# Output projections of the FFNs and the mLSTM: one 512-column product for both activation parts in place of two of 256 columns

## The chip, the cores and the metric

The kernel runs on one core of one Trainium2 chip. The metric is the device time of one execution in microseconds. The kernel before was run three times; the median is 1103.17 us (1102.94 to 1103.98).

## The reference

The reference is a two-layer network on 256 tokens of width 1024. Each layer has three sub-layers, and each sub-layer adds its gated output to the residual stream `x`; shift, scale and gate come from a modulation vector that is computed from the condition `c`.

```python
mod = (c_act @ ada_w[layer] + ada_b[layer]).reshape(bsz, N_SUB, 3, D_MODEL)[:, :, :, None, :]
def modulate(t, sub):
    return rms_norm(t, norm_g[layer, sub]) * (1.0 + mod[:, sub, 1]) + mod[:, sub, 0]
h = modulate(x, 0)
x = x + HALF_STEP * (1.0 + mod[:, 0, 2]) * swiglu(h, ffn_w_gate[layer, 0], ffn_w_up[layer, 0], ffn_w_down[layer, 0])
h = modulate(x, 1)
...
x = x + (1.0 + mod[:, 1, 2]) * y.astype(x.dtype)
h = modulate(x, 2)
x = x + HALF_STEP * (1.0 + mod[:, 2, 2]) * swiglu(h, ffn_w_gate[layer, 1], ffn_w_up[layer, 1], ffn_w_down[layer, 1])
```

`y` is the output of a hybrid mixer (a recurrent unit and a state-space block) in the first layer, and of an mLSTM block in the second. `swiglu` is `(silu(h @ w_gate) * (h @ w_up)) @ w_down` with an inner width of 2816. Everything is float32. The change touches the last product of four FFNs, `... @ w_down` (2816 to 1024), and that of the mLSTM (2048 to 1024).

## The kernel before

**Layout.** Activations lie with features on partitions and the 256 tokens (T) along the free axis. A width of 1024 is 8 chunks (ND) of 128 features, the FFN's inner width 22 (NF). The sub-layers have numbers s = 0 to 5: FFN, hybrid, FFN, FFN, mLSTM, FFN.

**Precision.** Each float32 factor is split into an upper and a lower part of the program's type fp32r. Activations are split into a tile `both` of shape [128, 2, 256]: `both[:, 0]` is the upper part, `both[:, 1]` the lower one, one behind the other in memory (L359, L360). Weights come as pieces of eight 128x128 tiles, 512 KB each: a DMA on SP's queue brings `wraw`, ScalarE casts it to `whi` (L99), VectorE subtracts and leaves `wlo` (L100). Pieces are made four ahead of their use; four raw buffers and six pairs of parts hold them. A weight tile then takes three products (`multiply`): upper weights by upper activations (L372), upper weights by lower activations (L373), lower weights by upper activations (L374). All three have 256 columns and add up in one half of a bank of 512 float32 columns. Each product loads its weights anew (a LDWEIGHTS on the row called PEld, beside the product before it).

**Output projection** (`out_project`). For the FFNs and the mLSTM it runs over eight output chunks d; each takes one of four banks (`mm_bank`), `project` runs over all input tiles (22 tiles `ph` in an FFN, 16 tiles `yb` in the mLSTM), and then:

- VectorE scales the bank by the gate and adds it to `x` (L492),
- ScalarE squares the new `x` (L349), VectorE adds up the squares (L353),
- ScalarE and VectorE make the next sub-layer's input from `x` times its scale, split into two parts `hb` (L418, L419).

The hybrid (s = 1) takes another path of the same function, through `banks`, which the change leaves alone. VectorE also computes the modulation: blocks `ada` of 128x1024 (L230) are handed out over the weight pieces by a table.

**Start of the next sub-layer** (`begin`). The first 32 weight tiles of a sub-layer are multiplied with the not yet normalised input (258 columns, L434 to L436), while the norm is made: products of one column sum the squares (`rst_n`, L317), VectorE computes the reciprocal root (L283 to L292), TensorE spreads it (`rsb_n`, L340), and VectorE and ScalarE write the normalised `hb` (L402 to L405). `rst_n` needs the square of the last chunk of `x`, so the last chunk of a projection stands ahead of the next norm.

**Order.** The program is traced in the order of the code; a scheduler then decides the order on each engine. Each engine executes its own list in order, and waits at an instruction whose inputs are not there.

Of the kernel before, what the change touches and what calls it, by code (L numbers as in the profile page):

```python
# [15 lines left out]
ALU = mybir.AluOpType  # L16
# [4 lines left out]
T = 256  # L21
D = 1024
ND = D // P
# [111 lines left out]
def body(ctx: ExitStack, tc: tile.TileContext, a, out, dbg=None):  # L135
    nc = tc.nc
# [21 lines left out]
    def mm_bank(name):  # L158
        return ps_mm.tile([P, 512], F32, tag="mm", name=name)
# [18 lines left out]
    xs_t = [xall[:, k, :] for k in range(ND)]  # L178
# [23 lines left out]
    for b in range(2):  # L202
        q = fpool.tile([P, D], F32, tag="xsq", name=f"xsq{b}")
        squares = nc.vector.scalar_tensor_tensor(out=q, in0=xn[:, b], scalar=1.0, in1=xn[:, b], op0=ALU.mult,
                                                 op1=ALU.mult, accum_out=ss_in[:, b:b + 1])
# [40 lines left out]
    W = Weights(tc, a["wst"], rawp, partp, pump)  # L246
# [14 lines left out]
    def mod_gate(s, f):  # L261
        m = mods[s]
        o = COL["ada_b"] + 24 * s + 16
        g = modp.tile([P, 8], F32, tag="gate", name=f"gate{s}")
        nc.vector.tensor_tensor(out=g, in0=m[:, 16:24], in1=cols[:, o:o + 8], op=ALU.add)
        nc.vector.tensor_scalar(out=g, in0=g, scalar1=1.0, scalar2=f, op0=ALU.add, op1=ALU.mult)
        return g
# [101 lines left out]
    def multiply(dst, both, start, stop):  # L369

        wh, wl = W.next()
        m = nc.tensor.matmul(dst, wh, both[:, 0, :], start=start, stop=False, skip_group_check=True)  # L372
        nc.tensor.matmul(dst, wh, both[:, 1, :], start=False, stop=False, skip_group_check=True)  # L373
        nc.tensor.matmul(dst, wl, both[:, 0, :], start=False, stop=stop, skip_group_check=True)  # L374
        return m

    def project(dst, rhs):

        for k, both in enumerate(rhs):
            last = multiply(dst, both, k == 0, k == len(rhs) - 1)  # L380
        return last
# [27 lines left out]
    def scale_shift_columns(s):  # L409
        sh, _ = mod_shift_scale(s)  # L410
        shb = sh.unsqueeze(2).to_broadcast([P, 8, 2])
        nc.vector.tensor_copy(hh[:, :, T:T + 2], shb)
        nc.vector.tensor_tensor(out=hl[:, :, T:T + 2], in0=shb, in1=hh[:, :, T:T + 2].bitcast(F32), op=ALU.subtract)
# [42 lines left out]
    def out_project(s, rhs, half, beside=None):  # L456


        acc = [xp.tile([P, T], F32, tag=f"ssq{s % 2}", name=f"ssq{s}")]
        banks = []  # L460
        if isinstance(rhs, tuple):

            *early, rhs = rhs
            for n, (part, lo, hi) in enumerate(early):
                for d in range(ND):
                    if n < 2:
                        beside(n, d)
                    if n == 0:
                        if d % 2 == 0:
                            bank = mm_bank(f"od{s}_{d}")  # L470
                        banks.append(bank[:, d % 2 * T:(d % 2 + 1) * T])
                    dst = banks[d]
                    for k, both in enumerate(part[lo:hi]):

                        m = multiply(dst, both, n == 0 and k == 0 and d % 2 == 0, False)
                        if n == 0 and k == 0:
                            if d % 2 == 0:
                                head = m
                            else:
                                tc.add_manual_dep(m.ins, head.ins.name, NOSYNC, reason="one start per bank")  # L480
            rhs = rhs[0][rhs[1]:rhs[2]]
        for n, d in enumerate(LAST_ORDER if banks else range(ND)):
            if banks:
                dst = banks[d]
                for k, both in enumerate(rhs):
                    multiply(dst, both, False, k == len(rhs) - 1)
            else:
                dst = mm_bank(f"od{s}_{d}")[:, 0:T]
                project(dst, rhs)
            if n == 0:  # L490
                g = mod_gate(s, 0.5 if half else 1.0)
            nc.vector.scalar_tensor_tensor(out=xs_t[d], in0=dst, scalar=g[:, d:d + 1], in1=xs_t[d],  # L492
                                           op0=ALU.mult, op1=ALU.add)
            last_act = [add_square(acc, xs_t[d], n, ND, f"o{s}_{d}")]
            if s < 5:
                if n == 0:
                    scale_shift_columns(s + 1)
                scale_chunk(s + 1, d)
            elif d == 5:
                root = small.tile([P, 1], F32, tag="root", name="root", bufs=1)  # L500
                with tc.issue_after(last_act[0]):
                    nc.scalar.activation(root, eps, AF.Sqrt)
            if dbg is not None:
                nc.gpsimd.dma_start(dbg[f"x{s}"][d], xs_t[d])
        return acc
# [793 lines left out]
    rs, _ = rsqrt_act(sum_tokens(acc, "fin", "mm")[:, 0:2], "fin")  # L1299
    banks = [ax_bank(f"fin{i}", ("ax", "ax", "p", "q")[i]) for i in range(4)]  # L1300
# [5 lines left out]
    for lo in (0, 512):  # L1306
        for b in range(2):
            dst, src = res[:, b, lo:lo + 512], banks[2 * (lo // 512) + b]
# [113 lines left out]
```

## Time and profile before

| | |
|---|---|
| median of three runs | 1103.17 us |
| the profiled execution, its span | 1102.1 us |
| instructions in the span | 23364 |
| VectorE's differences `wlo` (L100) | 366, 445.4 us |
| ScalarE's casts `whi` (L99) | 364, 379.7 us |
| read from memory | 269.77 MB |

The span is the time from the first to the last instruction that the profiler saw; the time of a run is about 1.1 us longer. In the profile PE is TensorE's products, PEld its weight loads, DVE is VectorE, ACT ScalarE, SP the engine that issues the weight DMAs. Rows read: line of the code, engine, operation, result and inputs by their names in the program, shape and count; then busy time in us and mean duration in ns. A product's duration runs from its start until its last result is written, and products overlap; the pace is read from start to start. By start times the projections lie at 136 to 196 us (s = 0), 492 to 552 (s = 2), 674 to 734 (s = 3), 868 to 912 (s = 4) and 1033 to 1093 (s = 5).

### The profile page before, as it was taken

The numbers are of one execution on the slowest core, as the hardware profiler recorded it, in microseconds if no ns is written. First come the engines' busy times: TensorE is split into PE (matmuls) and PEld (weight loads), VectorE is DVE, ScalarE is ACT, GpSimd is POOL, SyncE is SP. The second block draws the span as 40 slices with busy tenths as digits, with TensorE's granted clock in tenths as the row PEclk, the third lists the DMA queues.
The fourth block names the chain that finished last, engine by engine and source line by source line (L and its number), as shares of the span: only waits on it lengthen the run. The fifth ranks groups of instructions, "written<-read, shape, count | busy, mean of one in ns | idle before, by whom it ended". The sixth has DMA issues, their size and how long they took to land.

```text
span 1102.1 us, 23364 instructions
## 1 busy us (share of the span) xinstructions
PE 1087.0 (99%) x9350; PEld 1073.5 (97%) x9350; DVE 919.7 (83%) x1651; ACT 642.5 (58%) x1051; POOL 9.4 (1%) x29
## 2 busy tenths in 40 slices
PE   8999999999999999999999999999999999999997
PEld 6999999999999999999999999999999999999997
DVE  7999998999999899989699988869778868766552
ACT  5665455677986665454554554548776655544452
POOL 0000000000000000000000000010000000000000
PEclk9999999999999999999999999999999999999999
DMA  9889998655845489999848998853432664775551
GB/s 371 329 304 388 359 384 339 193 192 191 287 159 182 152 298 369 355 344 329 281 164 317 335 328 308 311 203 116 146 95 93 201 193 164 265 234 197 194 173 39
DMA packets 74990, 272.34 MB, mean 247 GB/s; under 512 B 8417, under 2 KB 8577, under 8 KB 74882
## 3 DMA queue, kind: packets, MB, share of 16 engines
q1 hardware_dynamic: 74304, 269.49, 69.8%
q0 software_dynamic: 432, 1.10, 0.4%
q8 instruction: 73, 1.20, 0.4%
q14 instruction: 35, 0.29, 0.1%
q10 hardware_dynamic: 146, 0.27, 0.1%
HBM read 269.77 MB, written 1.05 MB: 246 GB/s over the span
## 4 chain that ended last, share of the span: by engine, by line
PE 81%; DVE 12%; ACT 2%; DMA 2%; issue 2%; SPq 0%; DVEq 0%; ACTq 0%
PE gu L373 13%; PE gu L374 13%; PE gu L372 13%; PE od L373 9%; PE od L372 9%; PE od L374 9%; DVE wlo L100 4%; DMA wraw<-in_wst_dram 1%; PE zz L373 1%; PE zz L374 1%; PE zz L372 1%; PE gu_f L434 1%; PE gu_f L436 1%; PE gu_f L435 1%; DVE ada L230 1%
## 5 line engine op out<-in xcount | busy, mean ns | idle before, releaser
L100 DVE TENSOR_TENSOR wlo<-wraw,whi 128x1024 fp32r<-128x1024 f32 x366 | 445.4, 1220 | 95.2 <-ACT whi L99 93.9
L99 ACT CAST whi<-wraw 128x1024 fp32r<-128x1024 f32 x364 | 379.7, 1049 | 229.4 <-PE od L373 71.4
L373 PE MATMUL gu<-hb,whi 128*128 128x256 f32 x1312 | 361.0, 276 | 0.4 <-DVE hb L569 0.4
L374 PE MATMUL gu<-hb,wlo 128*128 128x256 f32 x1312 | 360.7, 276 | 0.0
L372 PE MATMUL gu<-hb,whi 128*128 128x256 f32 x1312 | 358.5, 277 | 1.8 <-ACT hb L404 1.1
L372 PEld LDWEIGHTS gu<-hb,whi 128*128 128x128 f32 x1312 | 244.5, 188 | 2.8 <-ACT hb L404 1.3
L373 PEld LDWEIGHTS gu<-hb,whi 128*128 128x128 f32 x1312 | 246.3, 188 | 0.8 <-DVE hb L569 0.8
L374 PEld LDWEIGHTS gu<-hb,wlo 128*128 128x128 f32 x1312 | 246.3, 188 | 0.0
L372 PE MATMUL od<-ph,whi 128*128 128x256 f32 x704 | 194.3, 276 | 0.0
L373 PE MATMUL od<-ph,whi 128*128 128x256 f32 x704 | 194.3, 276 | 0.0
L374 PE MATMUL od<-ph,wlo 128*128 128x256 f32 x704 | 194.3, 276 | 0.0
L230 DVE SCALAR_TENSOR_TENSOR ada<-ada,cact 128x1024 f32<-128x1024 f32 x144 | 175.1, 1217 | 1.3 <-DMA ada<-in_adaT_dram 1.3
L374 PEld LDWEIGHTS od<-ph,wlo 128*128 128x128 f32 x704 | 132.2, 188 | 0.0
L372 PEld LDWEIGHTS od<-ph,whi 128*128 128x128 f32 x704 | 132.2, 188 | 0.0
L373 PEld LDWEIGHTS od<-ph,whi 128*128 128x128 f32 x704 | 132.2, 188 | 0.0
L359 ACT CAST ph<-fg 128x256 fp32r<-128x256 f32 x88 | 35.1, 408 | 106.2 <-DVE fg L516 106.2
L360 DVE TENSOR_TENSOR ph<-fg,ph 128x256 fp32r<-128x256 f32 x88 | 36.3, 420 | 12.1 <-ACT ph L359 12.1
L492 DVE SCALAR_TENSOR_TENSOR x<-od,gate,x 128x256 f32<-128x256 f32 x48 | 23.0, 481 | 26.4 <-PE od L374 26.4
L349 ACT ACTIVATE sq_o<-x 128x256 f32<-128x256 f32 x42 | 17.6, 418 | 41.4 <-DVE x L492 41.2
L373 PE MATMUL zz<-hb,whi 128*128 128x256 f32 x128 | 36.2, 283 | 0.0
L372 PE MATMUL zz<-hb,whi 128*128 128x256 f32 x128 | 36.2, 283 | 0.0
L374 PE MATMUL zz<-hb,wlo 128*128 128x256 f32 x128 | 36.2, 283 | 0.0
(412 smaller groups left out, 1948.2 us busy)
## 6 DMA issues: line engine op xcount, KB each, us to landing
wraw<-in_wst_dram SPq DMA_DIRECT2D x366, 512.0 KB, 4.6
ada<-in_adaT_dram SPq DMA_DIRECT2D x144, 512.0 KB, 5.9
xn<-in_x_dram SPq DMA_DIRECT2D x2, 512.0 KB, 4.0
wgr<-in_ml_wg_dram POOLq DMA_DIRECT2D x3, 256.0 KB, 3.0
out_dram<-res SPq DMA_DIRECT2D x3, 256.0 KB, 2.4
out_dram<-res ACTq DMA_DIRECT2D x1, 256.0 KB, 2.8
cols<-in_cols_dram SPq DMA_DIRECT2D x1, 226.0 KB, 7.6
wkr<-in_ml_wkr_dram POOLq DMA_DIRECT2D x1, 128.0 KB, 2.3
```

The source lines that it names most:

```text
L99: raw_hi = nc.scalar.copy(hi, raw)
L100: self.last = nc.vector.tensor_tensor(out=lo, in0=raw, in1=hi.bitcast(F32), op=ALU.subtract)
L230: return nc.vector.scalar_tensor_tensor(out=raw, in0=raw, scalar=1.0, in1=cact, op0=ALU.mult, op1=ALU.mult, accum_out=mods[s][:, m:m + 1])
L349: square = nc.scalar.activation(q, x, AF.Square).ins
L359: nc.scalar.copy(hi, src)
L360: nc.vector.tensor_tensor(out=both[:, 1, :], in0=src, in1=hi.bitcast(F32), op=ALU.subtract)
L372: m = nc.tensor.matmul(dst, wh, both[:, 0, :], start=start, stop=False, skip_group_check=True)
L373: nc.tensor.matmul(dst, wh, both[:, 1, :], start=False, stop=False, skip_group_check=True)
L374: nc.tensor.matmul(dst, wl, both[:, 0, :], start=False, stop=stop, skip_group_check=True)
L434: nc.tensor.matmul(dst, wh, rh, start=(k == 0), stop=False)
L435: nc.tensor.matmul(dst, wh, rl, start=False, stop=False)
L492: nc.vector.scalar_tensor_tensor(out=xs_t[d], in0=dst, scalar=g[:, d:d + 1], in1=xs_t[d], op0=ALU.mult, op1=ALU.add)
```

## The change

A new helper, `multiply_wide`, takes a whole bank. One product of upper weights by both parts of the activation (512 columns) leaves the upper parts' sum in the bank's left half and the lower parts' sum in its right half; a second product adds lower weights by upper activations to the left half. In `out_project` the first seven chunks of an FFN's or the mLSTM's projection use it; the eighth chunk stays with `multiply`. After each of the seven chunks VectorE adds the right half to `x`, in one more instruction with the same gate, and then the left half as before.

```diff
--- before.py
+++ after.py
@@ -374,6 +374,13 @@
         nc.tensor.matmul(dst, wl, both[:, 0, :], start=False, stop=stop, skip_group_check=True)
         return m
 
+    def multiply_wide(bank, both, start, stop):
+
+        wh, wl = W.next()
+        nc.tensor.matmul(bank.rearrange("p (i t) -> p i t", i=2), wh, both, start=start, stop=stop,
+                         skip_group_check=True)
+        nc.tensor.matmul(bank[:, 0:T], wl, both[:, 0, :], start=False, stop=stop, skip_group_check=True)
+
     def project(dst, rhs):
 
         for k, both in enumerate(rhs):
@@ -484,11 +491,19 @@
                 dst = banks[d]
                 for k, both in enumerate(rhs):
                     multiply(dst, both, False, k == len(rhs) - 1)
+            elif n < ND - 1:
+                wide = mm_bank(f"od{s}_{d}")
+                dst = wide[:, 0:T]
+                for k, both in enumerate(rhs):
+                    multiply_wide(wide, both, k == 0, k == len(rhs) - 1)
             else:
                 dst = mm_bank(f"od{s}_{d}")[:, 0:T]
                 project(dst, rhs)
             if n == 0:
                 g = mod_gate(s, 0.5 if half else 1.0)
+            if not banks and n < ND - 1:
+                nc.vector.scalar_tensor_tensor(out=xs_t[d], in0=wide[:, T:2 * T], scalar=g[:, d:d + 1], in1=xs_t[d],
+                                               op0=ALU.mult, op1=ALU.add)
             nc.vector.scalar_tensor_tensor(out=xs_t[d], in0=dst, scalar=g[:, d:d + 1], in1=xs_t[d],
                                            op0=ALU.mult, op1=ALU.add)
             last_act = [add_square(acc, xs_t[d], n, ND, f"o{s}_{d}")]
```

The lines move with it: what is L492 before is L507 after, and the added addition is L505; the wide product is L380, the product with the lower weights behind it L382; L418/L419 are L425/L426.

On TensorE the first FFN's projection shows what happens to the products, here two tiles of chunk 1 before (`od0_1` is the bank of chunk 1 of sub-layer 0, `ph0_4` the fifth input tile, `whi47` and `wlo47` piece 47 of the weights):

```order
L372 MATMUL od0_1_1976<-ph0_4_828,whi47_1832 128x256
L373 MATMUL od0_1_1976<-ph0_4_828,whi47_1832 128x256
L374 MATMUL od0_1_1976<-ph0_4_828,wlo47_1833 128x256
L372 MATMUL od0_1_1976<-ph0_5_834,whi47_1832 128x256
L373 MATMUL od0_1_1976<-ph0_5_834,whi47_1832 128x256
L374 MATMUL od0_1_1976<-ph0_5_834,wlo47_1833 128x256
```

The same place on TensorE after the change, three tiles:

```order
L380 MATMUL od0_1_1955<-ph0_3_822,whi47_1832 128x512
L382 MATMUL od0_1_1955<-ph0_3_822,wlo47_1833 128x256
L380 MATMUL od0_1_1955<-ph0_4_828,whi47_1832 128x512
L382 MATMUL od0_1_1955<-ph0_4_828,wlo47_1833 128x256
L380 MATMUL od0_1_1955<-ph0_5_834,whi47_1832 128x512
L382 MATMUL od0_1_1955<-ph0_5_834,wlo47_1833 128x256
```

A tile has two products in place of three, the order of tiles and pieces is the same. Four FFNs with seven chunks of 22 tiles and the mLSTM with seven chunks of 16 tiles make 728 tiles that change.

On VectorE the end of the same projection, around the addition of chunk 6, before (`wlo65` is the difference of piece 65, `ada62` a modulation block, `hb` the next input):

```order
L100 TENSOR_TENSOR wlo65_2474<-wraw65_2471,whi65_2473 128x1024
L492 SCALAR_TENSOR_TENSOR x_104<-od0_6_2458,gate0_1962,x_104 128x256
L100 TENSOR_TENSOR wlo66_2504<-wraw66_2501,whi66_2503 128x1024
L230 SCALAR_TENSOR_TENSOR ada62_2507,mod2_1836<-ada62_2507,cact_117 128x1024
L353 TENSOR_TENSOR ssq0_1870<-ssq0_1870,sq_o0_6_2550 128x256
L419 SCALAR_TENSOR_TENSOR hb_106<-x_104,scale1_1968,hb_106 128x256
```

The same place on VectorE after the change:

```order
L505 SCALAR_TENSOR_TENSOR x_104<-od0_6_2332,gate0_1940,x_104 128x256
L100 TENSOR_TENSOR wlo65_2344<-wraw65_2341,whi65_2343 128x1024
L507 SCALAR_TENSOR_TENSOR x_104<-od0_6_2332,gate0_1940,x_104 128x256
L100 TENSOR_TENSOR wlo66_2366<-wraw66_2363,whi66_2365 128x1024
L230 SCALAR_TENSOR_TENSOR ada62_2369,mod2_1836<-ada62_2369,cact_117 128x1024
L353 TENSOR_TENSOR ssq0_1870<-ssq0_1870,sq_o0_6_2403 128x256
L426 SCALAR_TENSOR_TENSOR hb_106<-x_104,scale1_1947,hb_106 128x256
```

There are two additions now, and the difference of piece 65, which stood ahead of the addition, stands between them.

A little further on VectorE, at the addition of chunk 7, the last, and the norm behind it (`rsv`, `rsy` and `rsw` are the root's chain), before:

```order
L100 TENSOR_TENSOR wlo68_2577<-wraw68_2574,whi68_2576 128x1024
L492 SCALAR_TENSOR_TENSOR x_104<-od0_7_2555,gate0_1962,x_104 128x256
L100 TENSOR_TENSOR wlo69_2607<-wraw69_2604,whi69_2606 128x1024
L419 SCALAR_TENSOR_TENSOR hb_106<-x_104,scale1_1968,hb_106 128x256
L329 TENSOR_SCALAR rsv_n1_2667<-rst_n1_2662 128x2
L723 TENSOR_SCALAR dt_3199<-cols_105 128x8
L283 TENSOR_SCALAR rsy_n1_2670<-rsv_n1_2667 128x2
L286 TENSOR_TENSOR rsw_n1_2669<-rsy_n1_2670 128x2
```

The same place on VectorE after the change:

```order
L507 SCALAR_TENSOR_TENSOR x_104<-od0_7_2408,gate0_1940,x_104 128x256
L738 TENSOR_SCALAR dt_3052<-cols_105 128x8
L100 TENSOR_TENSOR wlo68_2430<-wraw68_2427,whi68_2429 128x1024
L426 SCALAR_TENSOR_TENSOR hb_106<-x_104,scale1_1947,hb_106 128x256
L329 TENSOR_SCALAR rsv_n1_2520<-rst_n1_2515 128x2
L283 TENSOR_SCALAR rsy_n1_2523<-rsv_n1_2520 128x2
L100 TENSOR_TENSOR wlo69_2460<-wraw69_2457,whi69_2459 128x1024
L286 TENSOR_TENSOR rsw_n1_2522<-rsy_n1_2523 128x2
```

The difference of piece 68 moved behind the last addition, and that of piece 69 into the root's chain. SP's list of weight and modulation loads differs in one place, where one weight load and one modulation load have changed places.

## The prediction

> **What bounds the kernel now.** I read the page's busy shares first, then its clock line, then the chain of work that ended last, then PE's waits.
>
> ```profile
> PE 1087.0 (99%) x9350; PEld 1073.5 (97%) x9350; DVE 919.7 (83%) x1651; ACT 642.5 (58%) x1051; POOL 9.4 (1%) x29
> PEclk9999999999999999999999999999999999999999
> PE 81%; DVE 12%; ACT 2%; DMA 2%; issue 2%; SPq 0%; DVEq 0%; ACTq 0%
> L372 PE MATMUL od<-ph,whi 128*128 128x256 f32 x704 | 194.3, 276 | 0.0
> L372 PE MATMUL od<-yb,whi 128*128 128x256 f32 x128 | 35.3, 276 | 0.0
> ```
>
> TensorE is busy for 99% of the span and 81% of the chain; the clock is at full speed in every slice. The last two rows are the products that the change touches (a third of them: L373 and L374 have as many). Their idle time is 0.0, so nothing makes them wait. The kernel is bound by PE, and in these stages by the number and pace of products, not by weights or VectorE.
>
> A matmul's listed duration (276 ns) contains its pipeline; what counts is the distance from one start to the next. From the timelines of PE and of its weight loads in the first projection:
>
> ```profile
> 160.18 0.28 PE L372 MATMUL od<-ph,whi 128*128 128x256 f32 x1
> 160.29 0.28 PE L373 MATMUL od<-ph,whi 128*128 128x256 f32 x1
> 160.41 0.28 PE L374 MATMUL od<-ph,wlo 128*128 128x256 f32 x1
> ...
> 163.92 0.28 PE L372 MATMUL od<-ph,whi 128*128 128x256 f32 x1
> 160.18 0.19 PEld L373 LDWEIGHTS od<-ph,whi 128*128 128x128 f32 x1
> 160.30 0.19 PEld L374 LDWEIGHTS od<-ph,wlo 128*128 128x128 f32 x1
> ```
>
> From 160.18 to 163.92 there are 33 products (11 tiles): 3.74/33 = 113.3 ns each, **340.0 ns per tile**. Every product has a load of its own, which begins with the product before it.
>
> **What sets the 113.3 ns?** Products of other shapes tell: four float32 lines of the mLSTM in the chain, and one-column products in PE's timeline:
>
> ```profile
> 779.92 0.93 PE v L1069 x8
> 780.85 0.86 PE q L1076 x4
> 781.71 1.78 PE s L1088 x8
> 197.13 0.60 PE L317 MATMUL rst_n<-ones,sq_o 128*128 128x1 f32 x4
> 197.60 0.58 PE L317 MATMUL rst_n<-ones,ssq 128*128 128x1 f32 x4
> ```
>
> v has 136 columns and takes 0.93/8 = 116 ns; q has 256 and takes 0.86/4 = 215 ns; s has 264 and takes 1.78/8 = 222.5 ns. q's 256 columns take 1.9 times as long as the projection's 256, which I read as two passes over them. From v to q that is 99 ns for 240 column passes, 0.4125 ns each; 256 columns in one pass therefore stream in about 105.6 ns, plus a fixed part of 215/2 - 105.6 = 1.9. The two rows of rst_n (197.13 to 197.60 for four) show that products of one column still take 0.47/4 = 118 ns. So a 256-column product of the projection, at 113.3, is held by the load of its weights more than by its columns, by a margin of a few ns. A 512-column pass is as many passes as one q product: **215 ns (estimate from q)**, long enough to hide a load.
>
> **The change on PE.** 4 FFN projections x 7 chunks x 22 tiles = 616 tiles, and 7 x 16 = 112 in the mLSTM: **728 tiles**. Each loses one product and one load; its moving columns stay 768. The new pair is 215 ns for the wide product, with the load of wlo under it, then a 256-column product with the next tile's load under it. If that one stays at 113.3, the pair is 328.3, a gain of 11.7 ns per tile. But rows behind products that were bound by their stream show another pace:
>
> ```profile
> 262.04 1.02 PE L804 MATMUL st<-xw,bnat 128*128 128x512 f32 x2
> ...
> 263.01 0.28 PE L373 MATMUL xl<-hb,whi 128*128 128x256 f32 x1
> ...
> 264.80 0.28 PE L373 MATMUL xl<-hb,whi 128*128 128x256 f32 x1
> ```
>
> After the wide float32 products at 262.04 the same 256-column products run at (264.80 - 263.01)/15 = 119 ns, where the projection has 113.3. In the new tile every narrow product stands behind a wide one, so I take 119 for it: 215 + 119 = **334 ns per tile, 6 ns less than 340**. The bounds: 328 from below (113.3 stays), 344 from above (215 with 5 more for the load beside it, as the narrow ones show, and 124 as the slowest spacing, twice the same 5 over 113.3). 728 x 6.0 ns = 4.4 us gained, from 8.5 us to a loss of 2.9.
>
> **The change on VectorE.** 5 stages x 7 = 35 more scaled additions. Each chunk's first addition waits for the last product of its bank, as the old one did; the second follows it. What VectorE has free, by stage (columns: us; then busy PE, PEld, DVE, ACT, POOL with counts; clock, DMA share, GB/s):
>
> ```profile
> core 0: us, PE busy (x) PEld busy (x) DVE busy (x) ACT busy (x) POOL busy (x), PEclk, DMA share, GB/s
> 136.00:184.00 48.00, 48.00 (x426) 48.00 (x426) 46.80 (x71) 26.67 (x35) 0.00 (x0) 1.00 1.00 381
> 184.00:209.00 25.00, 24.99 (x215) 24.78 (x214) 20.28 (x45) 9.90 (x18) 0.98 (x3) 1.00 0.72 244
> 209.00:339.00 130.00, 127.85 (x1130) 124.74 (x1129) 127.28 (x257) 111.45 (x216) 0.00 (x0) 1.00 0.59 195
> 492.00:552.00 60.00, 60.00 (x532) 60.00 (x531) 48.11 (x69) 29.25 (x38) 1.07 (x2) 1.00 0.90 312
> 868.00:912.00 44.00, 44.00 (x391) 44.00 (x390) 31.20 (x41) 23.20 (x33) 0.00 (x0) 1.00 0.67 215
> 1033.00:1093.00 60.00, 60.00 (x532) 60.00 (x531) 27.14 (x33) 25.60 (x35) 0.00 (x0) 1.00 0.37 125
> 188.60 0.48 DVE L492 SCALAR_TENSOR_TENSOR x<-od,gate,x 128x256 f32<-128x256 f32 x1 [2.85 <-PE od L374]
> 189.00 1.22 DVE L100 TENSOR_TENSOR wlo<-wraw,whi 128x1024 fp32r<-128x1024 f32 x1
> ```
>
> An addition takes 0.40 us to the next start, so seven take 2.8 us. In the three later projections shown VectorE is idle for 12, 13 and 33 us: 2.8 us are hidden there, and I cost them at nothing; without that cover they would be 2.8 us per stage. The bank is held 0.4 us longer, and four banks of 7.5 us each cover it. The stages whose cover is thin are the first projection (VectorE 46.8 of 48) and the hybrid behind it (127.28 of 130). The additions eat the 2.85 us of idle time at 188.60; in the new order one weight difference less stands ahead of the first addition of od_6 and ahead of that of od_7, and wlo69, which stood ahead of the root's chain, now stands inside it. In the hybrid VectorE has almost nothing free, and so what PE gains in the first projection it loses there: 7 x 22 x 6.0 ns = **0.9 us of the gain goes**. At worst all of 2.8 us return, at best nothing.
>
> The end of the first projection is the place where a late VectorE reaches PE:
>
> ```profile
> 196.08 0.48 DVE L492 SCALAR_TENSOR_TENSOR x<-od,gate,x 128x256 f32<-128x256 f32 x1 [0.17 <-PE od L374]
> 196.48 1.22 DVE L100 TENSOR_TENSOR wlo<-wraw,whi 128x1024 fp32r<-128x1024 f32 x1
> 196.83 0.28 PE L436 MATMUL bc<-hb,wlo 128*128 128x258 f32 x1
> ```
>
> The last addition began at 196.08, after 0.17 us of waiting for its bank; ScalarE squares what it leaves, and rst_n (197.13, above) comes 0.30 us after the product before it instead of 0.12: rst_n is already the square that PE waits for. Between the additions of od_6 and od_7 the order has as many weight differences and modulation blocks as before, and one addition more: 0.40 less the 0.17 of idle time makes the last addition **0.2 us** late, and PE with it. Behind it a weight difference of 1.22 us now stands inside the root's chain; PE has the begin's products to do meanwhile (96 of 0.12 us), so I cost it at nothing; 1.2 is the upper bound of the term. ScalarE's cast, SP's queue of weight loads and the order on both stay as they are but for a swap of one weight load with one modulation load on SP. The last chunk of each stage keeps three products, so the other stages' ends keep their form.
>
> **The sum**: -4.4 + 0.9 + 0.2 = -3.3 us. The profiled span is 1102.1; the median of the runs is 1103.17, so 1.1 us lie around the span, which I leave: 1103.2 - 3.3 = **1099.9 us**.
>
> The page "TensorE: Matmul & The Clock Gate" of the Trainium skill, section "LDWEIGHTS (loading the stationary operand)", gives a load as its columns divided by 1.2 ns, 106.7 for 128; that speaks for loads as the pace, and for a narrow product that keeps it; the 119 behind wide products speaks against taking that for the whole. By the page's load alone, with the 6.6 ns that the trace has above it (113.3), the tile would be 328, and the sum that of the first rival.
>
> **The rivals.**
>
> *The narrow product stays at 113.3.* The pair is 328.3 and the gain 11.7 ns. For it: the load begins with the product before it, however that came to start. Against it: the 119 in the xl rows. All 728 tiles give 8.5 us, less 1.8 for the first projection (154 x 11.7) and 0.2 more at its end: -6.5, so 1096.7; with nothing lost, 1094.7.
>
> *Only a fixed cost per product goes.* Products would be bound by columns, at 113.3 per 256, and a wide one would take twice that less the fixed part, 1.9 ns by the q row. 728 x 1.9 = 1.4 us, less 0.3 for the first projection and 0.2 at its end: -0.9, so 1102.3, which is no change. Against it stand 215 for 512 passes in q, 11.6 less than 226.6. The same page, section "Back-to-back issue gap", has columns divided by 2.4 plus 2.5 ns for a product; by that rule three products of 256 are 327.5 and the new pair 325.0, a gain of 2.5 ns and 1.8 us; the trace's 113.3 instead of 109.2 speaks against that rule at 256 columns.
>
> *The change doesn't shorten anything*: each half of the wide product takes what a narrow product takes (113.3), and nothing is gained: +0.2 at the end of the first projection, 1103.4.
>
> *A load beside a wide stream slows both (slower).* The wide product reads two kilobytes per partition while wlo is read for the array; if it takes 220 and the narrow one 124, the pair is 344. 728 x 4 ns = +2.9, and 0.2 at the end of the first projection: 1106.3. It decides from a pair of 340 ns on. For it: 119 against 113.3 shows that loads and streams do disturb each other. Against it: q's and s's loads lie beside their streams too, at 0.4125 ns per column pass.
>
> **How the numbers follow.** Forecast (pair of 332 to 337): 0.42. Narrow stays at 113.3: 0.24. Only the fixed cost: 0.13. Nothing at all: 0.07. Slower: 0.14. A measurement of this kernel can tell about 0.2%, 2.2 us, from no change. Faster by more than that: 0.24 and 0.32 of the forecast, 0.56. Within it: 0.13, 0.07 and 0.08 of the forecast (pairs over 335.5), 0.28. Slower: 0.16, with 0.02 of the forecast for the first projection's upper bounds. The forecast's own range, pairs of 332 to 337 with a fifth lost in the first projection and 0.2 at its end, is 1098.8 to 1101.7. The range goes from the first rival's 1094.7, rounded to 1095.0, up to just short of the slow one's 1106.3: 1106.0.
>
> **What would show it.** In PE's timeline of a projection, the distance from a wide product to the narrow one behind it (215 expected) and from there to the next wide one (119; 113 for the first rival, 124 for the last). A chunk of 22 tiles should take 7.35 us, 7.48 before. At the end of the first projection rst_n should start 0.5 us after the product before it, 0.30 before; VectorE's busy time in the hybrid should stay at 127 us in a stretch as long as before or longer. PE's od stages must still show no idle time: idle time there, ahead of a product on a free bank or on wlo, would make the prediction wrong, as would a pair over 340 ns or a hybrid that gets shorter.

## The result, and the profile after

The changed kernel takes 1111.45 us (1111.21 to 1112.09, 4 runs), the kernel before 1103.58 beside it (1102.94 to 1104.02): a ratio of 1.0075, with a 95% interval of 1.0061 to 1.0089. The change makes the kernel slower by 7.9 us; 3.3 us faster was forecast, and the range ended at 1106.0.

The page of the kernel after, the busy shares, the chain by engine and the groups of the new products:

```profile
PE 1097.3 (99%) x8622; PEld 1051.7 (95%) x8622; DVE 935.4 (84%) x1686; ACT 642.9 (58%) x1051; POOL 9.4 (1%) x29
PEclk9999999999999999999999999999999999999999
PE 86%; DVE 9%; ACT 2%; issue 1%; DMA 1%; SPq 0%; DVEq 0%; ACTq 0%
L380 PE MATMUL od<-ph,whi 128*128 128x512 f32 x616 | 215.0, 393 | 0.0
L382 PE MATMUL od<-ph,wlo 128*128 128x256 f32 x616 | 172.7, 280 | 0.0
L380 PE MATMUL od<-yb,whi 128*128 128x512 f32 x112 | 39.1, 393 | 0.0
```

The page shows 728 products and 728 loads fewer, as it should (9350 and 8622), the clock at full speed, and no idle time ahead of the new products. PE waits for nothing new in the projections, and yet its share of the chain grew. So the time is in the products. PE's timeline of the kernel after, in the same chunk as before:

```profile
159.62 0.40 PE L380 MATMUL od<-ph,whi 128*128 128x512 f32 x1
159.85 0.28 PE L382 MATMUL od<-ph,wlo 128*128 128x256 f32 x1
159.97 0.40 PE L380 MATMUL od<-ph,whi 128*128 128x512 f32 x1
160.21 0.28 PE L382 MATMUL od<-ph,wlo 128*128 128x256 f32 x1
160.33 0.40 PE L380 MATMUL od<-ph,whi 128*128 128x512 f32 x1
...
162.77 0.39 PE L380 MATMUL od<-ph,whi 128*128 128x512 f32 x1
```

From 159.62 to 162.77 there are nine pairs, 350 ns each, where three narrow products took 340.0. Over all 728 pairs of the trace the mean distance from a wide product to its narrow one is **230.3 ns**, and from there to the next wide one **118.4**: a tile takes 348.7. The forecast had 215 and 119.

Where the time went, from the first to the last product of each projection, and what lies between (us, worked out from the start times of both traces):

| | before | after | difference |
|---|---|---|---|
| projections of s = 0, 2, 3, 5, each | 59.73 | 61.17 | +1.44, four times |
| projection of the mLSTM | 43.41 | 44.38 | +0.97 |
| from the projection of s = 0 to the hybrid's first product `y` | 103.20 | 103.03 | -0.17 |
| from there to the hybrid's projection (250 products) | 24.50 | 25.80 | +1.30 |
| the hybrid's projection and all the rest | | | -0.15 |
| span | 1102.13 | 1109.85 | +7.72 |

Five projections give +6.7, and 728 x 8.7 ns = 6.3 of that are the pairs. The rest is the last chunk of each projection, whose three narrow products per tile run at 114 to 125 ns, mostly 117 to 119, behind the wide ones. In the four FFNs this lasts for 18 products, up to the end of the weight piece, and in the mLSTM for three; behind that they are at 113.3 again.

The stretch from the first projection to the hybrid's is 1.14 us longer in sum. VectorE's timeline of the kernel after at chunk 6 of the first projection, and PE's at the norm:

```profile
189.83 0.48 DVE L505 SCALAR_TENSOR_TENSOR x<-od,gate,x 128x256 f32<-128x256 f32 x1 [1.39 <-PE od L382]
190.23 1.22 DVE L100 TENSOR_TENSOR wlo<-wraw,whi 128x1024 fp32r<-128x1024 f32 x1
191.36 0.48 DVE L507 SCALAR_TENSOR_TENSOR x<-od,gate,x 128x256 f32<-128x256 f32 x1
198.16 0.28 PE L443 MATMUL bc<-hb,wlo 128*128 128x258 f32 x1
198.57 0.27 PE L317 MATMUL rst_n<-ones,sq_o 128*128 128x1 f32 x1
```

VectorE stands idle for 1.39 us ahead of the addition, with a weight difference waiting behind it that stood ahead of it before; rst_n comes 0.41 us after the product before it, 0.30 before. This is not where the 1.14 us are lost: at the hybrid's first product `y`, more than 100 us later, the kernel after has taken 0.17 us less than the kernel before. They are lost in the last 25 us ahead of the hybrid's projection, where the order on PE has changed too. `y` are products of the state-space block with 128 columns, `gl` products of the hybrid with 256. PE's timeline there before:

```profile
304.07 0.66 PE L900 MATMUL y<-mt,ssd 128*64 128x128 f32 x8
304.56 0.39 PE L900 MATMUL y<-ce,ssd 128*64 128x128 f32 x4
304.78 0.61 PE L900 MATMUL y<-mt,ssd 128*64 128x128 f32 x8
305.21 0.39 PE L900 MATMUL y<-ce,ssd 128*64 128x128 f32 x4
305.53 0.39 PE L373 MATMUL gl<-hb,whi 128*128 128x256 f32 x1
```

and after:

```profile
305.12 0.66 PE L915 MATMUL y<-mt,ssd 128*64 128x128 f32 x8
305.70 0.39 PE L372 MATMUL gl<-hb,whi 128*128 128x256 f32 x1
305.93 0.28 PE L373 MATMUL gl<-hb,whi 128*128 128x256 f32 x1
306.14 0.44 PE L915 MATMUL y<-ce,ssd 128*64 128x128 f32 x4
...
307.16 0.39 PE L374 MATMUL gl<-hb,wlo 128*128 128x256 f32 x1
```

The 24 products `y` of a group took 1.46 us in one go. Now two `gl` stand among them, and the group takes 2.04 us; the two `gl` would explain 0.24 of the difference at their usual 0.12. Three of the four groups of `y` are split in this way (8 and 16, 8 and 16, 2 and 22).

### The profile page after: what moved, and what is told of

It reads as the page before. It is cut to its first block, busy times and chain, and to the rows that moved or that the text cites. A ratio compares the mean times of both kernels' runs of the same rounds, so it can differ in the third digit from the quotient of the medians.

```text
span 1109.9 us, 21950 instructions
## 1 busy us (share of the span) xinstructions
PE 1097.3 (99%) x8622; PEld 1051.7 (95%) x8622; DVE 935.4 (84%) x1686; ACT 642.9 (58%) x1051; POOL 9.4 (1%) x29
## 4 chain that ended last, share of the span: by engine, by line
PE 86%; DVE 9%; ACT 2%; issue 1%; DMA 1%; SPq 0%; DVEq 0%; ACTq 0%
PE od L380 15%; PE gu L373 13%; PE gu L374 13%; PE gu L372 13%; PE od L382 8%; DVE wlo L100 3%; PE od L373 2%; PE od L372 2%; PE od L374 2%; DVE ada L230 2%; PE zz L373 1%; PE zz L374 1%; PE zz L372 1%; PE gu_f L441 1%; PE gu_f L443 1%
## 5 line engine op out<-in xcount | busy, mean ns | idle before, releaser
L100 DVE TENSOR_TENSOR wlo<-wraw,whi 128x1024 fp32r<-128x1024 f32 x366 | 445.8, 1223 | 88.5 <-ACT whi L99 86.7
L380 PE MATMUL od<-ph,whi 128*128 128x512 f32 x616 | 215.0, 393 | 0.0
L382 PE MATMUL od<-ph,wlo 128*128 128x256 f32 x616 | 172.7, 280 | 0.0
L380 PEld LDWEIGHTS od<-ph,whi 128*128 128x128 f32 x616 | 116.0, 188 | 25.9
L382 PEld LDWEIGHTS od<-ph,wlo 128*128 128x128 f32 x616 | 115.8, 188 | 0.0
L380 PE MATMUL od<-yb,whi 128*128 128x512 f32 x112 | 39.1, 393 | 0.0
L531 DVE TENSOR_TENSOR fg<-fg,gu 128x256 f32<-128x256 f32 x82 | 33.7, 416 | 1.4 <-ACT fg L530 1.4
L530 ACT ACTIVATE fg<-gu 128x256 f32<-128x256 f32 x82 | 30.5, 377 | 6.7 <-PE gu L374 6.7
```

Of the source, the lines that this page charges most:

```text
L100: self.last = nc.vector.tensor_tensor(out=lo, in0=raw, in1=hi.bitcast(F32), op=ALU.subtract)
L380: nc.tensor.matmul(bank.rearrange("p (i t) -> p i t", i=2), wh, both, start=start, stop=stop, skip_group_check=True)
L382: nc.tensor.matmul(bank[:, 0:T], wl, both[:, 0, :], start=False, stop=stop, skip_group_check=True)
L530: nc.scalar.activation(g, b[:, 0:T], AF.Silu)
L531: nc.vector.tensor_tensor(out=g, in0=g, in1=b[:, T:2 * T], op=ALU.mult)
```

## The experiments

The question: what makes a wide product 230 ns, and does anything but the pair cost time? The first four kernels ran on one chip. The first gave each projection another form of the pair (cut to the essential, as the other code below):

```diff
 nc.tensor.matmul(bank[:, 0:T], wl, both[:, 0, :], ...)          # s = 0: as the change
+nc.tensor.matmul(bank[0:32, 0:T], wl[:, 0:32], both[:, 0, :], ...)   # s = 2
+wh, full = wh[:, 0:32], full[0:32]                                # s = 3, behind the first tile of a chunk
+nc.tensor.matmul(full, wl, both, ...)                             # mLSTM
+multiply_grouped(wide, rhs)                                       # s = 5
```

> One look; each projection has its own form. Sub-layer 0: as the change. Sub-layer 2: the lower weights' product has only 32 output columns, so its load beside the wide product is short (left out: the lower weights' share of 96 of 128 outputs). Sub-layer 3: the wide product has only 32 output columns after the first tile, so its load beside the narrow product is short (left out: most of the sum for 96 of 128 outputs). mLSTM: both products 512 columns wide (adds lower weights by lower activations). Sub-layer 5: eight wide products of a piece, then its eight narrow ones. The changed kernel had 230.3 ns for a wide product and 118.4 for a narrow one. Theory LOAD (a load beside a stream slows the stream): sub-layer 2 wide about 215, narrow 117 to 119; sub-layer 3 wide 229 to 233, narrow about 107; mLSTM 229 to 233 for each; sub-layer 5 wide 229 to 233 and narrow 113 to 117. Theory COLUMN (each column of this format takes 0.443 ns or more, whatever the load does): sub-layer 2 wide 227 to 233 still; mLSTM 227; sub-layer 5 227 and 113. Theory CHANGE (going from wide to narrow and back costs about 4 ns each way): sub-layer 2 as now, 229; mLSTM 227 or less; sub-layer 5 within groups 227 or less and 113, a tile at 340 or less.

The trace of this kernel in sub-layer 2, the weight loads and the products (the shape behind the names is rows by output columns, then rows by moving columns):

```profile
500.24 0.19 PEld L405 LDWEIGHTS od<-ph,whi 128*128 128x128 f32 x1
500.36 0.11 PEld L409 LDWEIGHTS od<-ph,wlo 128*32 128x32 f32 x1
500.36 0.39 PE L405 MATMUL od<-ph,whi 128*128 128x512 f32 x1
500.58 0.28 PE L409 MATMUL od<-ph,wlo 128*32 128x256 f32 x1
500.70 0.39 PE L405 MATMUL od<-ph,whi 128*128 128x512 f32 x1
500.93 0.28 PE L409 MATMUL od<-ph,wlo 128*32 128x256 f32 x1
501.05 0.40 PE L405 MATMUL od<-ph,whi 128*128 128x512 f32 x1
```

The load of the lower weights shrank from 0.19 to 0.11 us, and the wide product beside it still takes 231.6 ns on average (154 of them). With short loads beside the narrow products (s = 3) these take 117.7. The other forms: 512 columns for both products 232.6 and 230.3; eight wide ones in a row 231.0, eight narrow ones in a row 116.7. LOAD falls as a price that grows with the load's length. So does CHANGE, since wide products in a row aren't cheaper.

The second kernel moved the weight buffers:

```diff
-PLACES = (("wloa", 320), ("whia", 448), ("whic", 448), ("wlob", 448), ("whib", 64), ("wloc", 64))
+PLACES = (("wloa", 128), ("whia", 192), ("whic", 256), ("wlob", 256), ("whib", 0), ("wloc", 0))
```

> The change with the six weight buffers at other places, modulo 512 bytes, against the activations: lower parts at 128, 256 and 0 where they were at 320, 448 and 64; upper parts at 192, 256 and 0 where they were at 448, 64 and 448 or so. Other stages may change too; only the projections are read. Theory LOAD with conflicts of addresses: the pair changes by several ns between the three kinds of pieces and against the 346.7 and 353.3 of now. COLUMN and CHANGE: 346.7 for every kind, within 1 ns.

The pairs took 343 to 359 ns. By kind of piece (three pairs of buffers, a, b and c, take turns) they took 350.9, 352.6 and 353.2 on average, against 346.8, 352.8 and 347.0 in the change: the places matter, by a few ns. (The activations moved too, so that the offsets in the expectation were off by 64 bytes.) The whole kernel took 1137.0 us in its one run. The FFNs' projections, at 61.7 us each, explain little of that: the ordinary triples of 256 columns elsewhere lost their pace, as the eighth run shows below.

The third kernel has VectorE's part of the change without the wide product:

```diff
-nc.tensor.matmul(bank.rearrange("p (i t) -> p i t", i=2), wh, both, ...)
+nc.tensor.matmul(bank[:, 0:T], wh, both[:, 0, :], ...)
+nc.tensor.matmul(bank[:, T:2 * T], wh, both[:, 1, :], ...)
```

> Three narrow products as before, but the lower activations' product goes to the bank's right half, and VectorE adds both halves as in the change: its part without the wide product. If the wide product is the whole loss: projections at 113.3 ns per product as before, 59.7 us each, and 0 to +1.5 us in all, from VectorE in the first projection and the hybrid (the changed kernel's stretch between these was 1.1 us longer). If the additions or the half banks cost PE: more than +2 us, with waits of PE in the projections.

1103.31 us against 1103.11 for the kernel before on that chip, ratio 1.0000 (0.9992 to 1.0009). All five projections are as long as before (59.73 and 43.41), and the stretch to the hybrid's projection 127.77. Its groups of `y` are whole, as before. The 35 additions and the use of both halves of a bank cost nothing that can be measured.

The fourth kernel is the change with the products of a piece in groups:

```diff
+for i, both, wh, wl in group:   # eight tiles of one piece
+    nc.tensor.matmul(wide.rearrange("p (i t) -> p i t", i=2), wh, both, ...)
+for i, both, wh, wl in group:
+    nc.tensor.matmul(wide[:, 0:T], wl, both[:, 0, :], ...)
```

> The change with eight wide products of a piece in a row, then its narrow ones, in all five projections. CHANGE: a tile at 340 or less, the time at 1103 or less, plus about 1 us for VectorE. LOAD: wide 229 to 233 and narrow 113 to 117, a tile at 342 to 350, +2 to +8 us. COLUMN: 227 and 113, a tile at 340, 0 to +1.5 us.

1110.77 us, ratio 1.0066 (1.0052 to 1.0079): as slow as the change within the intervals. Wide ones took 231.0 on average, narrow ones 116.5, a tile 347.6. In some groups the narrow ones were at 113 again from the second on; in others they stayed higher to the end, with the weights of the buffers b always (118.1 on average). So CHANGE and COLUMN, which had 340 per tile, don't fit; the range of LOAD (342 to 350) does, though by the first kernel the load's length is not the reason.

Two kernels then measured products by their columns, with whole and with short loads, in other formats, and with each product starting its sum anew:

```diff
+wh, wl = wh[:, 0:c], wl[:, 0:c]            # c = 32 or 128 output columns
+nc.tensor.matmul(left, wh, both[:, 0, 0:t], start=start or fresh, ...)    # t = 128, 192 or 256
```

> One look, only the distances between products in each projection are read; after the first tile of a chunk parts of the sums are left out. Sub-layer 0: three narrow products (256 columns, as before the change) with weights cut to 32 output columns, so each load is short. Sub-layer 2: three products of 128 columns with whole weights. Sub-layer 3: the wide and narrow pair with weights cut to 32. mLSTM: three products of 128 columns with weights cut to 32. Sub-layer 5: the pair, with whole weights, each product starting its sum anew (no accumulation; only the last product of a chunk stays). The first look had wide products at 222 to 236 ns even beside a 32-column load. Theory COLUMN (a column of this format takes 0.443 ns without any load's help): sub-layer 0 113.3 still; sub-layer 2 held by loads, 107 to 113; sub-layer 3 227 and 113; mLSTM 57; sub-layer 5 230 and 118. Theory LOAD (the load sets 113.3, a column takes 0.417): sub-layer 0 about 107 to 109; sub-layer 2 113.3; sub-layer 3 215 and 107; mLSTM 54. Theory ACCUMULATE (adding to a bank costs the extra 6%): sub-layer 5 drops to 213 to 217 and 107 to 113, sub-layers 0 and 3 as COLUMN.

> One look, distances between products only; parts of the sums are left out. Sub-layer 0: three narrow products, each starting its sum anew. Sub-layer 2: three products of 192 columns with whole weights. Sub-layer 3: the wide product as plain float32 (two passes), narrow as now. mLSTM: the pair with weights cut to 32 output columns, each starting anew. Sub-layer 5: three products of 192 columns with weights cut to 32. COLUMN: sub-layer 0 113.3; sub-layer 2 107 to 113 (its loads); sub-layer 3 the wide product at 427 or less (0.417 per column and pass, as in the float32 lines of before); mLSTM 227 and 113; sub-layer 5 85. LOAD: sub-layer 0 113.3; sub-layer 2 113.3; sub-layer 5 80 or 81. ACCUMULATE: sub-layer 0 107 to 113, mLSTM 213 to 217 and 107.

Four lines each of the trace of the fifth kernel in sub-layer 0 (loads of 32 columns), and of the sixth in sub-layer 5 (32 columns, 192 moving):

```profile
160.04 0.28 PE L402 MATMUL od<-ph,whi 128*32 128x256 f32 x1
160.16 0.28 PE L403 MATMUL od<-ph,whi 128*32 128x256 f32 x1
160.27 0.28 PE L404 MATMUL od<-ph,wlo 128*32 128x256 f32 x1
160.38 0.28 PE L402 MATMUL od<-ph,whi 128*32 128x256 f32 x1
```

```profile
1129.95 0.25 PE L402 MATMUL od<-ph,whi 128*32 128x192 f32 x1
1130.04 0.25 PE L403 MATMUL od<-ph,whi 128*32 128x192 f32 x1
1130.13 0.25 PE L404 MATMUL od<-ph,wlo 128*32 128x192 f32 x1
1130.21 0.25 PE L402 MATMUL od<-ph,whi 128*32 128x192 f32 x1
```

From 160.04 to 160.38 is 0.34 us for three, 113.3 each, over all 434 distances of the stage: **with loads of 32 columns in place of 128 (records of 0.11 us for 0.19), the pace of the projection doesn't change at all**. From 1129.95 to 1130.21 is 0.26 us for three, 86.7 each: with fewer columns and short loads products are faster. In the sixth kernel's sub-layer 3 the wide product is plain float32:

```profile
681.27 1.02 PE L399 MATMUL od<-ph,whi 128*128 128x512 f32 x2
681.73 0.68 PE L404 MATMUL od<-ph,wlo 128*128 128x256 f32 x1
682.25 1.02 PE L399 MATMUL od<-ph,whi 128*128 128x512 f32 x2
```

Each such product leaves two records (x2), whose starts are 429 ns apart, and a tile takes 0.98 us. The seventh kernel completed the widths beyond 256.

```diff
+flat = both.rearrange("p i t -> p (i t)")
+nc.tensor.matmul(bank[0:c, 0:t], w[:, 0:c], flat[:, 0:t], ...)   # t = 512, 384, 320, 264
```

> One look, only distances between products are read; after the first tile of a chunk both products of a tile have the same width, and sums are left out or added that the reference has not. Widths: sub-layer 0 512 columns, weights cut to 32; sub-layer 2 384 columns; sub-layer 3 320; mLSTM 264 (these three with whole weights); sub-layer 5 384, weights cut to 32. Measured so far with short loads: 128 columns 60 ns (the commonest distance), 192 columns 86.7, 256 columns 113.3. In cycles of 0.4167 ns these are 144, 208 and 272, that is columns + 16. Theory FIXED (a product costs its columns and 16 cycles): 512 columns 220, 384 166.7, 320 140, 264 116.7. Theory COLUMN (17 cycles per 16 columns): 226.7, 170, 141.7, 116.9. Theory SPLIT (beyond 256 columns the 16 cycles are paid a second time): 226.7, 173.3, 146.7, 123.3. Distances up to 5 ns above these are seen after every disturbance; the smallest and the commonest values count. If the 230 of the change is set by the load, sub-layer 0 falls below it and sub-layer 5 below sub-layer 2.

Together, mean distances from start to start in ns, between products of one kind:

| moving columns | load 128 columns | load 32 columns |
|---|---|---|
| 128 | 110.8 | 60 (the commonest) |
| 192 | 111.3 | 86.7 |
| 256, all three equal | 113.3 | 113.3 |
| 264 | 122.2 | |
| 320 | 145.7 | |
| 384 | 176.3 | 174.5 |
| 512 | 231.4 | 231.5 |
| 512 as plain float32, from one record of a product to its second | 429 | |

Whole loads alone would allow 111 ns; the 256 columns take 113.3 whatever the load does. Up to 256 columns the products with short loads follow 0.417 ns per column and 6.7 per product (60.0, 86.7, 113.3). By FIXED 384 would take 166.7 and 512 220; they take 174.5 to 176.3 and 231. COLUMN lies 4 to 6 ns too low at every width beyond 256 (116.9, 141.7, 170, 226.7). SPLIT comes nearest: within about 1 ns at 264 (123.3) and 320 (146.7), 1 to 3 too low at 384 (173.3) and 5 too low at 512 (226.7). The load's length is worth 1.8 ns at 384 columns and nothing at 512. Starting sums anew changes nothing (113.3, and 230.3 and 118.4), so ACCUMULATE falls as well.

The eighth kernel moved the weight buffers once more, with the activations in place:

```diff
+PLACES = (("wloa", 96), ("whia", 224), ("whic", 288), ("wlob", 416), ("whib", 0), ("wloc", 64))
```

> The change, weight buffers moved again, this time with the activations at the same place as in the change (320 modulo 512 bytes). Against the activations the lower parts lie at 96, 416 and 64 (the last as in the change), the upper parts at 224, 0 and 288. Theory LOAD with addresses: a wide product with the lower part at 96 or 416 differs from 229.3 and 233.3 by 2 ns or more, at 64 it stays 229.3; a narrow one differs from 117.3 and 120. Theory without addresses (what is over 226.7 + 113.3 is a fixed price of going from wide to narrow and back): 346 to 349 per tile for every kind of piece.

Pairs of 347.2, 346.7 and 350.7 by kind of piece, and the whole kernel 1134.6 us in its one run. Against the change, b went from 352.8 to 346.7 and c from 347.0 to 350.7; a stayed, though its places moved as well. Its timeline in the first sub-layer's gate and up products, three narrow products per tile that the change doesn't touch:

```profile
90.00 0.29 PE L372 MATMUL gu<-hb,whi 128*128 128x256 f32 x1
90.12 0.28 PE L373 MATMUL gu<-hb,whi 128*128 128x256 f32 x1
90.24 0.28 PE L374 MATMUL gu<-hb,wlo 128*128 128x256 f32 x1
90.36 0.28 PE L372 MATMUL gu<-hb,whi 128*128 128x256 f32 x1
```

They take 120 here. The average over all 3936 gate and up products is 118.9 (119.2 in the second kernel), where the change and the kernel before have 114.2, waits included: 19 to 20 us of the 23 to 26 that these two kernels take beyond the change. So whether triples of equal products run at 113.3 hangs on the places of the weight buffers, too. It isn't those alone: in the last chunks of the second kernel's projections, with another input, triples come back to 113 with the moved buffers.

The ninth kernel tried some 35 places against each other, by reading weights from a shifted window:

```diff
+hi, lo = W.parts[i]
+wh, wl = hi[:, k * P + oh:k * P + oh + P], lo[:, k * P + ol:k * P + ol + P]
```

> The change with whole products, but seven of eight weight tiles are read from a shifted window of their piece (up to 127 columns later, so the sums are of the wrong weights; counts, sizes and order stay). Each chunk of each projection has its own shift, 0 to 384 bytes in steps of 16, 32 or 64, of the upper part, the lower part or both: some 100 combinations of places of the two loads against the stream. So far a pair took 346.7 or 353.3 ns for most pieces. Theory ADDRESS (where a load reads against where the stream reads sets what is over 340): pairs vary with the shift from about 340 to 355, some combinations at 340. Theory CADENCE (a wide product breaks the cadence that three equal products keep, wherever the loads read): no combination at 340, all at 346 to 354. Under both, none is below 340, since 768 columns at 17 cycles per 16 columns take 340.

Single pairs went from 340 to 361 ns (343 to 357 in the change), the means of a chunk from 346.5 to 352.7; six pairs of 728 took 340 and none less. A chunk mixes the three kinds of pieces, whose buffers lie at different places, so a combination of places is one piece in one chunk. One of them runs at 340. It is the piece in the buffers c in chunk 3 of sub-layer 0, with its lower part read 192 bytes later:

```profile
161.52 0.39 PE L394 MATMUL od<-ph,whi 128*128 128x512 f32 x1
161.74 0.28 PE L396 MATMUL od<-ph,wlo 128*128 128x256 f32 x1
161.86 0.39 PE L394 MATMUL od<-ph,whi 128*128 128x512 f32 x1
...
162.88 0.39 PE L394 MATMUL od<-ph,whi 128*128 128x512 f32 x1
```

From 161.52 to 162.88 are four pairs of 340 ns, 227 for the wide product and 113 for the narrow one; six pairs in a row took 340 or 341. In the 89 other combinations with four shifted pairs or more the mean was 346 or more. So ADDRESS holds, which had some combinations at 340, and CADENCE, which had none, falls: where the loads read moves what a pair takes beyond 340, here down to nothing. That combination was met in a single piece.

The tenth kernel went after the same price elsewhere, in the starts of the sub-layers, where products of 258 columns take 120 to 122:

```diff
-nc.tensor.matmul(dst, wh, rl, start=False, stop=False)
-nc.tensor.matmul(dst, wl, rh, start=False, stop=(k == ND - 1))
+nc.tensor.matmul(dst[:, 0:T], wh, rl[:, 0:T], start=False, ...)
+nc.tensor.matmul(dst[:, 0:T], wl, rh[:, 0:T], start=False, ...)
```

> Built on the kernel before, the output projections as there. In each sub-layer's start two of the three products per tile have 256 columns instead of 258: the upper part's product carries the shift's upper and lower part in its two extra columns, and a small addition sums them (left out: lower weights by the shift). 64 products in each of five starts lose two columns. If two columns over 256 cost a step of 6.7 ns as 258 columns at 120 suggest: 320 x 6.7 = 2.1 us, 1101 for 1103.2. If these products run at 118 to 120 because their cadence is disturbed, whatever their width: 0 to 0.6 us, no measurable change.

1102.59 against 1103.17, ratio 0.9997 (0.9988 to 1.0006): no measurable change. Without the waits (distances over 200 ns) the products of that stage came to 118.8 on average, 120.4 before. Those with 256 columns take 118.4 and those with 258 119.6, so the 120 were not a price of the two columns: among products of another width 256 columns don't come back to 113.3 either.

The last two kernels split the change by place:

```diff
-elif n < ND - 1:
+elif n < ND - 1 and s == 0:     # the eleventh; s > 0 in the twelfth; the additions likewise
```

> The wide products and their additions in sub-layer 0 alone. If the loss is the pair's price (348.7 for 340 ns) and, behind sub-layer 0, one weight difference that VectorE does later (the stretch from this projection to the hybrid's was 1.1 us longer in the change, and not longer where the halves were filled by narrow products): 1.4 + 1.1 = +2.5 us. If that 1.1 us came from elsewhere: +1.4.

> The wide products and their additions in sub-layers 2 to 5, sub-layer 0 as before. By the pair's price: 3 x 1.44 + 0.97 = +5.3 us, the stretch from sub-layer 0's projection to the hybrid's at 127.7 us as before. If the rest of the loss doesn't belong to sub-layer 0: +6.4.

Sub-layer 0 alone: 1106.07 against 1102.98, +3.1, ratio 1.0025 (1.0015 to 1.0035), with 61.17 us in the projection and 129.20 behind it: 1.44 + 1.50 = 2.9. All but sub-layer 0: 1108.22, +5.2, ratio 1.0045 (1.0032 to 1.0058), with 127.01 behind the first projection. Both agree with the price of the pair, and with a loss behind the first projection that belongs to the change in sub-layer 0. The two parts add up to 8.3 us, where the change measured 7.9.

That loss goes with the order on PE in the hybrid. With the split groups of `y`, the 250 products from the first `y` to the hybrid's projection take 25.65 us in the eleventh kernel and 25.80 in the first, fourth and ninth; with whole groups they take 24.44 in the third and 24.50 in the twelfth. The seventh kernel has products of 512 columns in sub-layer 0 but whole groups, and its stretch is not longer (126.73). The tenth has VectorE's order of before at chunk 6 but two of the three splits: there 247 products take 24.97 us. No run changed the order on PE alone.

## Why the prediction was wrong

**The bound was read rightly, its cause wrongly.** PE is the bound in the projections, before and after, and the number and pace of products set the time. The step that failed is "So a 256-column product of the projection, at 113.3, is held by the load of its weights more than by its columns". Short loads leave 113.3 as it is; whole loads alone would allow about 111. The columns hold it, by a margin of 1 to 3 ns over the loads, so hiding a load gains nothing.

**The term that was mis-sized** is "215 ns (estimate from q)" for the wide product: it measured 230.3. The estimate carried the pace of plain float32 over to a product in fp32r. In float32 a record of 512 columns takes 429 ns, twice the 215 of q, so the scaling by columns was right there; but each float32 product leaves two such records, and that a record is two passes is a reading that no run shows. Within fp32r the 256-column product itself gave a better base: two of them take 226.7. With that the premise that a product less is a gain goes as well: the best place that the runs met has 227 and 113, which is 340 as before.

**The narrow product behind it** was forecast at 119 from the xl rows and measured 118.4, so its size was right. That what stands before it sets this is true only in part: with the weights of the buffers b narrow products stay at 118 in a row, and in one piece of the ninth kernel they take 113 right behind wide ones. Beside the 340 of before, a pair loses 5.1 ns in the narrow product and 3.6 in the wide one.

**The upper bound of the pair**, 344, was too low: 348.7, a pair over 340 being a sign that the prediction itself named for its being wrong. It allowed 5 ns on a base of 215; on a base of two narrow products it would have been 226.7 + 5 + 124 = 355.7, and the range would have reached 1115. The rival that came nearest is a load beside a wide stream that slows both (1106.3). Its sign was right and its mechanism in part: the load's length plays no part at this width, but the place from which it reads moves a pair, from 353 by kind of piece down to 340. *The change doesn't shorten anything* had the wide product nearly right (226.7) and left out that the narrow one loses its pace.

**VectorE and the hybrid.** That 28 of the additions are hidden, that four banks cover the longer hold, and that nothing waits for weights was right: the kernel with all 35 additions and narrow products is at 1.0000. Of the two losses that the forecast put at the first projection, the 0.2 us at the norm measured 0.11 (0.41 for 0.30), and the 0.9 was part of a gain that didn't come. That they add up to nearly the 1.14 us measured is chance. Those lie in PE's order in the hybrid, a term that the prediction put at nothing without a reason: it and the section on the change look at the orders of SP, ScalarE and VectorE and at the projections, not at PE's order in the hybrid. That the split groups of `y` are the cause fits every run, but wasn't tried alone.

**The Trainium skill** (page "TensorE: Matmul & The Clock Gate", section "Back-to-back issue gap") gives columns divided by 2.4 plus 2.5 ns for an isolated product on a warm clock, which is 109.2 for 256 columns and 215.8 for 512. The runs show 113.3 and 224 to 241 in fp32r, so in this format products take longer than the rule gives. Its section "LDWEIGHTS (loading the stationary operand)", columns divided by 1.2, agrees in its slope: from 32 to 128 columns a load's record grows from 108 to 188 ns, 0.83 per column.

**Open**: why places of the weights against the activations cost a pair 6 to 13 ns, and why one of them costs nothing. It is not the load's length, not the addition to the bank, and not the alternation of widths.

## What to carry over

A shorter list of products is a gain only if the product that replaces them is cheaper than their sum; take its price from products of the same format, and where the trace has none of that width, take the sum of the products that it replaces as the first estimate (226.7 here, for 230.3) rather than a rate from another format (215). When two limits lie within 3 ns of each other (loads 111, columns 113.3), taking one away gains nothing: look for what the second one would allow before costing the first. A sequence that runs in an even pace may owe this to sizes and places that fit each other, and a change of either can cost more than it saves. After a change of one stage, compare the order on every engine in the stages behind it, too.

## What the runs showed of the hardware that was not expected

- Products in fp32r with 512 columns take on average longer than two with 256 (230 to 232 against 226.7), those with 320 and 384 about 146 and 174 to 176; up to 256 columns it is 0.417 ns per column and 6.7 per product.
- Where weights lie, modulo 512 bytes, sets the pace: the two kernels that moved the buffers took 1137.0 and 1134.6 us, with 118.9 to 119.2 per gate or up product instead of 114.2. A pair of a wide and a narrow product took 353 ns from some places, 347 from others, and 340 from one.
- Among products of another width, 256 columns take 118 to 120 instead of 113.3. In the change's last FFN chunks this lasts for 18 products behind the wide ones, until the next weight piece, in the mLSTM for three.
- Splitting a group of 24 products of 128 columns by two of 256 made it 0.34 us longer than the two alone explain (2.04 us for 1.46).
